# Row-wise infinity norm: another place in memory for the first tile, and a third store at the end

## The chip, the cores and the metric

The kernel runs on one core of a Trainium2 chip. The metric is the device time of one execution in microseconds (us). Before the change the median of three runs is 626.13 us (626.05 to 626.16).

## The reference

The input `x` is a matrix of 8192 x 8192 float32, 268 MB. The output is one float32 for each row, the largest absolute value in that row:

```python
return np.linalg.norm(x, ord=np.inf, axis=1)
```

Each element is read once; nothing but 32 KB is written.

## The kernel before

All arithmetic is done by VectorE: one instruction (`absmax`, L255 and L256) takes the largest absolute value along the free axis of a stretch of memory in SBUF. Everything else is loading: SyncE (SP) issues all loads, in one queue.

**Three regions of rows.** Each of the 128 partitions owns 64 rows of `x`. With `B = 2` rows a tile, a full tile is 128 partitions x 16384 elements, 64 KB a partition and 8 MB in all. Before the change the rows are split in two blocks of memory:

- The bulk, the first 38 x 128 rows. Partition p owns 38 adjacent rows, so neighbouring partitions lie 38 rows (1216 KB) apart in memory. It is loaded as 19 full tiles.
- The tail block, the last 26 x 128 rows. Partition p owns 26 adjacent rows, so neighbouring partitions lie 26 rows (832 KB) apart. Its first 24 rows are cut into 34 loads after the list `TAIL`: four full tiles, then smaller and smaller pieces down to 640 elements a partition. A piece may begin and end inside a row; then partial maxima are put in front of the piece that ends the row, and one more reduction joins them. The last 2 rows of this block (`x_f`) are the first tile of the whole kernel.

**Order.** The loop at L264 to L269 issues the first tile, then the 19 bulk tiles; the loop after L300 issues the 34 tail pieces. The tiles go round a ring of three slots in SBUF (`ring`, 3 x 16384 elements and some padding). A load into a slot waits until VectorE has reduced what was there, so at most three full tiles are in the ring. Loads are waited for with eight semaphores in rotation; a load or a store also waits for the former user of its semaphore.

**Results.** They are held in small tiles in SBUF: `r_bulk` (38 values a partition), `r_soon` (22 values, the tail's rows but its last two), and `r_late` (4 values: the tail's last two rows and the first tile's two). When the reductions of the load fourth from the end are done (L326), ScalarE issues the stores of `r_bulk` (L328) and `r_soon` (L330). SP issues the store of `r_late` (L332) after the last reduction. A tile `gap` pads the results, so that the ring begins at a multiple of 128 elements.

**Hand-made edges.** Four steps edit the finished program. `drop_implied_waits` removes waits that others imply. `start_first_load_early` puts the first load ahead of the opening barrier. `open_without_vector` takes VectorE out of that barrier. `finish_on_pool` lets GpSimd close the program: after the closing barrier it waits for the ScalarE stores' semaphores, clears the range of semaphores but for the one of the last store, waits for the last store, and resets that one by itself. It writes one clearing instruction for the semaphores below that one and one for those above; before the change none lies below. `SPARE` semaphores are allocated ahead of the others and not used; they move the numbers of the rest.

Of the kernel before, what the change touches and what calls it, by code (L numbers as in the profile page):

```python
# [12 lines left out]
F32 = mybir.dt.float32  # L13
# [4 lines left out]
HEAD, STEP = 32, 8  # L18
# [190 lines left out]
@with_exitstack  # L209
def kernel(  # L210
    ctx: ExitStack,
    tc: tile.TileContext,
    x: bass.AP,
    out: bass.AP,
    B: int = 2,
    SLOTS: int = 3,
    PAD: int = 128,
    SPARE: int = 12,
):
    nc = tc.nc  # L220
    P = nc.NUM_PARTITIONS
    rows, cols = x.shape
    W = B * cols
    R = SLOTS * W + PAD * 4


    n_tail = sum(w for _, w in TAIL) // cols
    met = 0
    for lo, w in sorted(TAIL):
        assert lo == met  # L230
        met += w
    assert met == n_tail * cols
    n_bulk_rows = rows // P - n_tail - B
    assert n_bulk_rows % B == 0
    N = n_bulk_rows // B + 1
    split = n_bulk_rows * P
    x_b = x[:split].rearrange("(p n b) c -> n p (b c)", p=P, b=B)
    out_b = out[:split].rearrange("(p n) -> p n", p=P)
    x_t = x[split:].rearrange("(p t) c -> p (t c)", p=P)
    out_t = out[split:].rearrange("(p t) -> p t", p=P)  # L240
    x_f = x_t[:, n_tail * cols :]

    for k in range(SPARE):
        nc.alloc_semaphore(f"spare{k}")
    pool = ctx.enter_context(tc.tile_pool(name="sbuf", bufs=1))
    r_bulk = pool.tile([P, n_bulk_rows], F32)
    n_soon = n_tail - 2
    r_soon = pool.tile([P, n_soon], F32)
    r_late = pool.tile([P, 2 + B], F32)
    used = [HEAD, n_bulk_rows, n_soon, 2 + B]  # L250
    gap = -sum(-(-n // STEP) * STEP for n in used) % PAD
    pool.tile([P, gap], F32, name="gap")
    ring = pool.tile([P, R], F32)

    def absmax(o, i):  # L255
        return nc.vector.reduce_max(  # L256
            out=o, in_=i, axis=X, apply_absolute_value=True
        )

    def after(ins, first, kind):  # L260
        info = mybir.DependencyInfo(kind, mybir.DependencyReason.SCHED_ONLY)
        tc.add_manual_dep(ins.ins, first.ins.name, info, reason="order")

    for n in range(N):  # L264
        at = n % SLOTS * W
        t = ring[:, at : at + W]
        nc.sync.dma_start(out=t, in_=x_f if n == 0 else x_b[n - 1])
        r = r_late[:, 2:] if n == 0 else r_bulk[:, (n - 1) * B : n * B]
        absmax(r, t.rearrange("p (b c) -> p b c", b=B))  # L269


    pieces = []
    for j, (at, w) in enumerate(TAIL):
        end = at + w
        while at < end:
            r = at // cols
            to = min(end, (r + 1) * cols)
            pieces.append((j, r, to - at))
            at = to
    of_row = [[k for k, s in enumerate(pieces) if s[1] == r] for r in range(n_tail)]  # L280


    def row_out(r):
        if r < n_soon:
            return r_soon[:, r : r + 1]
        return r_late[:, r - n_soon : r - n_soon + 1]

    here = N % SLOTS * W
    start, slot = [], []
    for j, (_, w) in enumerate(TAIL):  # L290
        first = next(s for s in pieces if s[0] == j)
        ks = of_row[first[1]]
        n_part = len(ks) - 1 if pieces[ks[-1]][0] == j else 0
        at = -(-(here + n_part) // PAD) * PAD
        if at + w > R:
            at = -(-n_part // PAD) * PAD
        start.append(at)
        slot.append(at - n_part)
        here = at + w

    for j, (src, w) in enumerate(TAIL):
        at = start[j]
        nc.sync.dma_start(out=ring[:, at : at + w], in_=x_t[:, src : src + w])
        if w == W and src % cols == 0:
            r = src // cols
            absmax(
                r_soon[:, r : r + B],
                ring[:, at : at + w].rearrange("p (b c) -> p b c", b=B),
            )
            continue  # L310
        here = [k for k, s in enumerate(pieces) if s[0] == j]
        offs = [at + sum(pieces[i][2] for i in here[:m]) for m in range(len(here))]
        todo = list(zip(here, offs))
        if slot[j] != at:

            todo = todo[1:] + todo[:1]
        for k, lo in todo:
            _, r, n = pieces[k]
            ks = of_row[r]
            if k == ks[-1]:  # L320
                frm = slot[j] if len(ks) > 1 else lo
                done = absmax(row_out(r), ring[:, frm : lo + n])
            else:
                to = slot[pieces[ks[-1]][0]] + ks.index(k)
                done = absmax(ring[:, to : to + 1], ring[:, lo : lo + n])
        if j == len(TAIL) - 4:  # L326

            ins = nc.scalar.dma_start(out=out_b, in_=r_bulk[:])  # L328
            after(ins, done, mybir.DependencyClass.Sync)
            ins = nc.scalar.dma_start(out=out_t[:, :n_soon], in_=r_soon[:])  # L330
            after(ins, done, mybir.DependencyClass.Sync)
    nc.sync.dma_start(out=out_t[:, n_soon:], in_=r_late[:])  # L332
    nc.at_finalize(drop_implied_waits)
    nc.at_finalize(start_first_load_early)
    nc.at_finalize(finish_on_pool)
    nc.at_finalize(open_without_vector)
# [30 lines left out]
```

## Time and profile before

| What | us |
|---|---|
| median of three runs | 626.13 |
| the profiled execution's own time | 626.09 |
| its span, first to last instruction | 623.5 |
| VectorE busy | 552.3 |
| VectorE waiting for loads, all groups | 70.3 |

The span is what the profile's times are counted in: 0 is the first instruction shown. A line of a group names the operation, what it writes and reads, the shape, how often, its busy time with the mean in ns, and the idle time of the engine just ahead of it with what ended that. The chain that ended last is followed back from the last instruction, at each step to what released it. For a DMA the profile gives the issue on the issuing engine's queue (SPq, ACTq) and the time from issue to landing. A window's row gives its length, the busy time of the engines, the granted TensorE clock, the mean share of the 16 DMA engines, and GB/s.

### The profile page before, as it was taken

The page shows a single profiled execution, that of the slowest core. Times are in us where ns is not written, and L with a number is a line of the kernel's source. Part 1 is how long each engine was busy: PE and PEld are TensorE (multiplying, and loading weights), DVE is VectorE, ACT ScalarE, POOL GpSimd, SP SyncE. Part 2 cuts the span into 40 slices and gives each one's busy share as a digit, 9 for nine tenths or more (in the row PEclk, how much of TensorE's full clock was granted, in tenths as well). Part 3 has the DMA queues.
Part 4 walks back from the last instruction along what each step waited for, and adds up shares of the span by engine and source line. Part 5 has one row for each costly group of instructions (what it writes and reads, how often), then busy time and mean ns, then how long its engine had stood idle before and what let it go on. Part 6 is the DMA issues. An engine that isn't in the chain of part 4 may idle for free.

```text
span 623.5 us, 152 instructions
## 1 busy us (share of the span) xinstructions
DVE 552.3 (89%) x64; POOL 0.2 (0%) x4
## 2 busy tenths in 40 slices
DVE  0588988889988899888898888988889999999999
POOL 0000000000000000000000000000000000000000
DMA  9999999999999999999999999999999999999998
GB/s 404 471 404 446 429 408 467 404 471 404 471 404 467 408 441 433 408 467 404 471 404 471 404 467 408 441 433 408 467 428 435 415 437 419 447 422 431 428 425 357
DMA packets 8065, 268.48 MB, mean 431 GB/s; under 512 B 1152, under 2 KB 1152, under 8 KB 2560
## 3 DMA queue, kind: packets, MB, share of 16 engines
q1 hardware_dynamic: 7776, 268.44, 99.7%
q10 hardware_dynamic: 288, 0.03, 0.0%
q14 instruction: 1, 0.01, 0.0%
HBM read 268.44 MB, written 0.03 MB: 431 GB/s over the span
## 4 chain that ended last, share of the span: by engine, by line
DMA 65%; DVE 35%; another core or an unknown queue 0%; issue 0%; DVEq 0%
DMA ring<-in_x_dram 65%; DVE r_bulk L256 19%; DVE r_soon L256 14%; DVE ring L256 1%; DVEq L362 0%; DVE r_late L256 0%
## 5 line engine op out<-in xcount | busy, mean ns | idle before, releaser
L256 DVE TENSOR_REDUCE r_bulk<-ring 128x2 f32<-128x16384 f32 x19 | 327.2, 17220 | 40.0 <-DMA ring<-in_x_dram 40.0
L256 DVE TENSOR_REDUCE r_soon<-ring 128x1 f32<-128x8192 f32 (+9 forms) x18 | 148.0, 8249 | 8.4 <-DMA ring<-in_x_dram 8.4
L256 DVE TENSOR_REDUCE ring<-ring 128x1 f32<-128x4992 f32 (+23 forms) x24 | 59.7, 2539 | 0.1
L256 DVE TENSOR_REDUCE r_late<-ring 128x2 f32<-128x16384 f32 (+2 forms) x3 | 18.9, 6329 | 21.9 <-DMA ring<-in_x_dram 21.9
L351 POOL MEMSET const-bfloat16-1.0<- 128x1 bf16 x1 | 0.1, 101 | 0.0
L351 POOL MEMSET const-uint8-127<- 128x1 uint8 x1 | 0.1, 101 | 0.0
L351 POOL MEMSET const-float32-0.0<- 128x1 f32 x1 | 0.1, 98 | 0.2 <-issue 0.2
L351 POOL MEMSET const-float32-1.0<- 128x1 f32 x1 | 0.1, 98 | 0.0
## 6 DMA issues: line engine op xcount, KB each, us to landing
ring<-in_x_dram SPq DMA_DIRECT2D x3, 4096.0 KB, 30.7
ring<-in_x_dram SPq DMA_DIRECT2D x2, 3744.0 KB, 38.6
ring<-in_x_dram SPq DMA_DIRECT2D x1, 6592.0 KB, 37.0
ring<-in_x_dram SPq DMA_DIRECT2D x1, 5696.0 KB, 31.1
ring<-in_x_dram SPq DMA_DIRECT2D x1, 4480.0 KB, 37.5
ring<-in_x_dram SPq DMA_DIRECT2D x1, 3328.0 KB, 42.5
ring<-in_x_dram SPq DMA_DIRECT2D x1, 2912.0 KB, 40.8
ring<-in_x_dram SPq DMA_DIRECT2D x1, 2592.0 KB, 38.3
```

The lines of the kernel that those rows point to most:

```text
L256: return nc.vector.reduce_max(out=o, in_=i, axis=X, apply_absolute_value=True)
L351: nc = _bacc.Bacc("TRN2", target_bir_lowering=False, num_devices=1)
```

## The change

The first tile is no longer taken from the end of the tail block. It is the first 256 rows of `x`: partition p takes rows 2p and 2p + 1, so the tile is one stretch of 8 MB. The bulk begins behind it and keeps 38 rows a partition. The tail block keeps only its 24 rows a partition, so that neighbouring partitions lie 24 rows (768 KB) apart. The first tile's results have a tile `r_first` and a store of their own; ScalarE issues it ahead of its two others. The final store has 2 values a partition and not 4. One spare semaphore fewer is allocated. As one more store takes a semaphore of the rotation, the final store gets the second of the eight and not the first; one semaphore then lies below it, and GpSimd's close has two clearing instructions.

```diff
-    SPARE: int = 12,
+    SPARE: int = 11,
...
-    n_bulk_rows = rows // P - n_tail - B
+    n_bulk_rows = rows // P - n_tail
     assert n_bulk_rows % B == 0
-    N = n_bulk_rows // B + 1
+    N = n_bulk_rows // B
     split = n_bulk_rows * P
-    x_b = x[:split].rearrange("(p n b) c -> n p (b c)", p=P, b=B)
-    out_b = out[:split].rearrange("(p n) -> p n", p=P)
+    x_f = x[: P * B].rearrange("(p b) c -> p (b c)", p=P)
+    out_f = out[: P * B].rearrange("(p b) -> p b", p=P)
+    x_b = x[P * B : split].rearrange("(p n b) c -> n p (b c)", p=P, b=B)
+    out_b = out[P * B : split].rearrange("(p n) -> p n", p=P)
     x_t = x[split:].rearrange("(p t) c -> p (t c)", p=P)
     out_t = out[split:].rearrange("(p t) -> p t", p=P)
-    x_f = x_t[:, n_tail * cols :]
...
-    r_bulk = pool.tile([P, n_bulk_rows], F32)
+    r_first = pool.tile([P, B], F32)
+    r_bulk = pool.tile([P, n_bulk_rows - B], F32)
...
-    r_late = pool.tile([P, 2 + B], F32)
-    used = [HEAD, n_bulk_rows, n_soon, 2 + B]
+    r_late = pool.tile([P, 2], F32)
+    used = [HEAD, B, n_bulk_rows - B, n_soon, 2]
...
-        r = r_late[:, 2:] if n == 0 else r_bulk[:, (n - 1) * B : n * B]
+        r = r_first[:] if n == 0 else r_bulk[:, (n - 1) * B : n * B]
...
         if j == len(TAIL) - 4:
 
+            ins = nc.scalar.dma_start(out=out_f, in_=r_first[:])
+            after(ins, done, mybir.DependencyClass.Sync)
             ins = nc.scalar.dma_start(out=out_b, in_=r_bulk[:])
             after(ins, done, mybir.DependencyClass.Sync)
```

## Prediction

> **What bounds the kernel now.** I read the page first: engines, DMA queues, the chain that ended last, the costliest group.
>
> ```profile
> DVE 552.3 (89%) x64; POOL 0.2 (0%) x4
> q1 hardware_dynamic: 7776, 268.44, 99.7%
> DMA 65%; DVE 35%; another core or an unknown queue 0%; issue 0%; DVEq 0%
> L256 DVE TENSOR_REDUCE r_bulk<-ring 128x2 f32<-128x16384 f32 x19 | 327.2, 17220 | 40.0 <-DMA ring<-in_x_dram 40.0
> ```
>
> The load queue keeps the 16 DMA engines busy for 99.7% of the span, VectorE is busy for 89%. In the bulk one 8 MB tile is reduced in 17.22 us, and VectorE then waits about 2.1 us (40.0 / 19) for the next load. The 35% of the chain on VectorE are no second limit: a load needs a free slot of the ring, so the chain is drawn through a reduction and then through two loads, while the queue stays full. The timeline gives the pace.
>
> ```profile
> 21.85 17.22 DVE L256 TENSOR_REDUCE r_late<-ring 128x2 f32<-128x16384 f32 x1 [21.85 <-DMA ring<-in_x_dram]
> 41.14 17.22 DVE L256 TENSOR_REDUCE r_bulk<-ring 128x2 f32<-128x16384 f32 x1 [2.07 <-DMA ring<-in_x_dram]
> ...
> 389.03 17.22 DVE L256 TENSOR_REDUCE r_bulk<-ring 128x2 f32<-128x16384 f32 x1 [2.15 <-DMA ring<-in_x_dram]
> ```
>
> Each of these reductions starts when its tile has landed, so the starts are landings. The first tile is there at 21.85, the twentieth (the last of the bulk) at 389.03: (389.03 - 21.85) / 19 = 19.33 us a tile, and 8.389 MB / 19.33 us = 434 GB/s. The end of the chain, in order of time, shows when the last load that the chain waits for is there and what is left after it:
>
> ```profile
> 609.80 11.17 DMA ring<-in_x_dram
> 620.98 0.04 issue
> 621.01 0.14 DVE r_late L256
> 621.15 0.61 issue
> 621.76 0.93 DVEq L362
> ```
>
> The tail is 24 rows a partition, as much as 12 tiles, and takes from 389.0 to 621.0: 232.0 / 12 = 19.33 us for 8 MB. So the bulk, whose partitions lie 38 rows (1216 KB) apart in memory, and the tail, whose partitions lie 26 rows (832 KB) apart, run at the same pace. A view of windows says what one row costs a DMA engine (columns: window, its length, VectorE, GpSimd, clock, DMA share, GB/s; a transfer counts whole in the window in which it starts, so a share may exceed 1):
>
> ```profile
> 0.98:1.90 0.92, 0.00 (x0) 0.00 (x0) 1.00 3.40 1140
> 60.00:80.00 20.00, 17.34 (x2) 0.00 (x0) 1.00 0.99 429
> 389.00:620.98 231.98, 223.44 (x43) 0.00 (x0) 1.00 1.00 429
> ```
>
> In the second row 429 GB/s x 20 us are 8.58 MB, or 131 pieces of 64 KB (two rows of x, what one partition takes of a tile); 0.99 x 16 engines x 20 us / 131 is 2.42 us a piece. In the first row 1140 x 0.92 is 1.05 MB, so 16 pieces, one on each engine, and 3.40 x 0.92 = 3.13 us for each. **Only the very first piece of each engine is slow**, by 0.71 us; everything later goes at the pace of an engine that never pauses.
>
> **The change, part by part.** The sum is made against the profiled execution: 626.09 us, span 623.5, so 2.6 us lie outside the span. The median of the runs is 626.13 (626.05 to 626.16); I take the 0.04 between them as nothing. About 0.2%, 1.25 us here, is what a measurement of this kernel can tell from no change.
>
> *Loads and reductions.* The same 54 loads of the same sizes in the same order, the same slots of the ring (the gap shrinks from 24 to 16 elements a partition as the results grow from 104 to 112, so the ring starts at 128 as before), the same 64 reductions with the same waits. Bytes: 268.44 MB as before, 32 tiles' worth at 19.33. Counted: 0 us. What changes is where a load reads.
>
> *First tile.* Its partitions now lie 64 KB apart, one stretch of 8 MB, and not 832 KB. No tile of the trace has this distance, so I bound it. Its landing at 21.85 follows the first issue, which the chain puts at 0.77, by 21.08 us; a tile of the full queue takes 19.33. The most that another place can give is thus 21.08 - 19.33 = 1.75 us (that also takes away the fixed way of issue and landing, which an address can hardly touch); more likely only the slow first piece, 0.71 us, depends on it. From the other side: were every piece of this tile as slow as the first, the 8 pieces of an engine would lose 7 x 0.71 = 5.0 us more. Both go straight to the end, since the queue is the limit and VectorE follows it. I take 0: 832 and 1216 KB gave the same pace, so the row nearest to it is the 2.42 us piece, and for the start the same 3.13 us.
>
> *Tail.* Its partitions lie 24 rows (768 KB) apart, not 832 KB. Not in the trace either. It can't gain: the engines were without pause at the pace that two other distances gave. The loss is bounded by the slowest piece shown: 232.0 x (3.13 / 2.42 - 1) = 68 us. I take 0, since 768 lies next to 832.
>
> [...]
>
> *The end.* ScalarE now issues three stores where it issued two, and the stores move one semaphore on. Timeline, then issue to landing:
>
> ```profile
> 620.20 0.38 ACTq L328 DMA_DIRECT2D out_dram<-r_bulk  x1
> 620.62 0.48 ACTq L330 DMA_DIRECT2D out_dram<-r_soon  x1
> 621.01 1.68 DVE L256 TENSOR_REDUCE r_late<-ring 128x1 f32<-128x773 f32 x2
> 622.72 0.35 SPq L332 DMA_DIRECT2D out_dram<-r_late  x1
> out_dram<-r_bulk ACTq DMA_DIRECT2D x1, 19.0 KB, 1.7
> out_dram<-r_soon ACTq DMA_DIRECT2D x1, 11.0 KB, 2.1
> out_dram<-r_late SPq DMA_DIRECT2D x1, 2.0 KB, 1.4
> ```
>
> Before: r_soon lands at 620.62 + 2.1 = 622.7, the final store at 622.72 + 1.4 = 624.1, which is past the span and ends the program. After: r_first at 620.20, and each later store one step of 0.42 on (620.62 - 620.20): r_bulk 620.62, r_soon 621.04, landing at 623.1; with the longer issue of 0.48 and its whole 0.48 again in landing, 623.7. That is 0.4 to 1.0 us ahead of the final store, whose issue at 622.72 hangs on VectorE alone. Behind the third store nothing is queued on ScalarE but the closing barrier, which SP joins last, after its own issue (622.72 + 0.35). The three stores wait for the earlier users of their semaphores, the loads of 1472, 1280 and 1152 elements; the reduction that releases the stores comes after all of those, so these waits are met. Its 128 pieces of 8 bytes now stand where r_bulk's 152 bytes stood beside the last load: fewer bytes, counted 0. If all cover were gone, one step would be on the path: +0.42 to +0.48. If r_first's 8-byte pieces saved the last load its company, VectorE would not notice, as it still works on the 773-element piece: no gain.
>
> *GpSimd's close.* The final store's semaphore now stands inside the range to be cleared, so there are two clearing instructions, not one. The nearest GpSimd row is
>
> ```profile
> L351 POOL MEMSET const-bfloat16-1.0<- 128x1 bf16 x1 | 0.1, 101 | 0.0
> ```
>
> 0.1 us, run while the final store is under way (1.4 us): 0, or 0.1 without that cover. Clearing comes after the waits for the other stores, at 623.1 to 623.7 by the above, so it still fits. The final store moves 8 bytes a partition, not 16, in as many pieces: between 0 and -0.1; I take 0, since 11 KB took 2.1 and 19 KB took 1.7, so bytes do not set it.
>
> **Sum:** 0 + 0 + 0 + 0 = 626.1 us, with terms of -0.7 to +0.5 that are plausible and far ends of -1.75 and +68.
>
> **Rivals.**
>
> *The first tile starts faster.* For it: 3.13 against 2.42 us is the one slow stretch of the whole queue, and the change touches its address. With 0.71 gone: 625.4, still inside 0.2%. With more than the piece gone, -1.25 to -1.75: 624.3 to 624.9. Against it: all engines start cold together whatever they read.
>
> *The third store ends the program.* r_soon's landing would have to take 1.0 us more than its 2.1. Then the close waits for it: 626.1 + 0.42 = 626.5 or so, inside 0.2%.
>
> *The tail's distance collides* (the other side). With 768 KB between partitions the engines, which step through their rows in time with each other, would ask the same part of the memory at once. It decides as soon as a 64 KB piece takes more than 2.42 us, because the load queue has no idle time to pay with. At the first tile's surplus, 1.75 us in each of 12 tiles, 647.1; at 3.13 us a piece, 626.1 + 68 = 694. Against it: neither 832 nor 1216 KB shows any of it.
>
> *The adjacent first tile collides.* Same mechanism in one tile only: up to 626.1 + 5.0 = 631.1, half of it 628.6.
>
> *The change does nothing to the addresses.* Excluded: the source distances differ in the built program.
>
> **How the numbers follow.** Forecast, 626.1: 0.42. First piece at full pace, 625.4: 0.12. Third store on the path, 626.5: 0.10. These three are within 0.2%: 0.64. First tile gains over 1.25: 0.10, so faster 0.10. Tail collides: 0.16; first tile collides: 0.10; slower 0.26. [...] The range goes from 624.3, the far end of the gain, to 628.6, half of the first tile's loss: 0.64 + 0.10 + about 0.05 = 0.79.
>
> **What would show it.** Right: first landing near 21.85, bulk and tail at 19.33 us for 8 MB, r_soon landed before the final store, ends within a few tenths. A first landing below 21.2 shows the faster start. Wrong: a tail that takes more than 233 us from the last bulk landing, with VectorE idle ahead of its r_soon groups; a first landing past 22.5; a final store that is not the last to land.

## The result, and the profile after

The changed kernel takes 627.39 us (median of 16 runs, 626.86 to 628.05), the kernel before 626.15 beside it (16 runs, 625.97 to 626.40). The ratio is 1.0021, with a 95% interval of 1.0014 to 1.0027: **slower by about 1.2 us**. The runs also scatter over 1.2 us, where those of before scatter over 0.4. The profiled execution took 627.54 us, 1.45 more than that of before, and its span is the same 623.5 us. So the loss lies past the last instruction shown. The other runs say the same: the time less the span is 3.2 to 4.4 us in the sixteen runs, and 2.6 to 2.7 in every run of the kernel before that was timed beside the experiments below.

The loads first, in the same windows as before the change:

```profile
0.98:1.90 0.92, 0.00 (x0) 0.00 (x0) 1.00 3.30 1140
60.00:80.00 20.00, 17.27 (x2) 0.00 (x0) 1.00 0.99 429
389.00:620.98 231.98, 223.42 (x43) 0.00 (x0) 1.00 1.00 429
```

A piece of 64 KB still takes 2.42 us, the first one of each engine 3.30 x 0.92 = 3.04 us where it took 3.13, and the tail has its 429 GB/s (the columns are window, length, VectorE, GpSimd, clock, share of the DMA engines, GB/s). The timeline agrees: landings at 21.97 and 389.05, where they were at 21.85 and 389.03.

```profile
21.97 17.22 DVE L258 TENSOR_REDUCE r_first<-ring 128x2 f32<-128x16384 f32 x1 [21.97 <-DMA ring<-in_x_dram]
...
389.05 17.22 DVE L258 TENSOR_REDUCE r_bulk<-ring 128x2 f32<-128x16384 f32 x1 [2.15 <-DMA ring<-in_x_dram]
```

The end, as issues on the queues (start, length) and as times from issue to landing:

```profile
620.22 0.38 ACTq L330 DMA_DIRECT2D out_dram<-r_first  x1
620.64 0.44 ACTq L332 DMA_DIRECT2D out_dram<-r_bulk  x1
621.03 1.68 DVE L258 TENSOR_REDUCE r_late<-ring 128x1 f32<-128x773 f32 x2
621.12 0.49 ACTq L334 DMA_DIRECT2D out_dram<-r_soon  x1
622.74 0.35 SPq L336 DMA_DIRECT2D out_dram<-r_late  x1
```

```profile
out_dram<-r_bulk ACTq DMA_DIRECT2D x1, 19.0 KB, 3.8
out_dram<-r_first ACTq DMA_DIRECT2D x1, 1.0 KB, 3.3
out_dram<-r_soon ACTq DMA_DIRECT2D x1, 11.0 KB, 4.2
out_dram<-r_late SPq DMA_DIRECT2D x1, 1.0 KB, 2.9
```

The issues stand where the prediction put them, within 0.1 us. The landings do not: r_bulk went from 1.7 to 3.8, r_soon from 2.1 to 4.2, and the final store from 1.4 to 2.9. It now lands at 622.74 + 2.9 = 625.6 and not at 624.1. These 1.5 us are the whole of the 1.45. The final store comes from SP's queue, not ScalarE's, moves half the bytes that it moved before, and is issued at the same time; that it is late because of a store ahead of it is what the experiments show. In the trace's records its sixteen engines used to report between 623.97 and 624.14; now the first does at 623.99 and the last at 625.59, 1.45 later.

So the lateness is not kept to one queue: the store on SP's took 2.9 us instead of 1.4. But a mere wait for r_first does not give the amount: r_first has landed at 620.22 + 3.3 = 623.5, and the three stores behind it land 0.9, 1.8 and 2.1 us after that.

### The profile page after: what moved, and what is told of

Same layout as the page of the kernel before. It is cut to its first block, busy times and chain, and to the rows that moved or that the text cites. A ratio compares the mean times of both kernels' runs of the same rounds, so it can differ in the third digit from the quotient of the medians.

```text
span 623.5 us, 153 instructions
## 1 busy us (share of the span) xinstructions
DVE 552.3 (89%) x64; POOL 0.2 (0%) x4
## 4 chain that ended last, share of the span: by engine, by line
DMA 65%; DVE 35%; another core or an unknown queue 0%; issue 0%; DVEq 0%
DMA ring<-in_x_dram 65%; DVE r_bulk L258 19%; DVE r_soon L258 14%; DVE ring L258 1%; DVEq L366 0%; DVE r_late L258 0%
## 5 line engine op out<-in xcount | busy, mean ns | idle before, releaser
L258 DVE TENSOR_REDUCE r_first<-ring 128x2 f32<-128x16384 f32 x1 | 17.2, 17220 | 22.0 <-DMA ring<-in_x_dram 22.0
L258 DVE TENSOR_REDUCE r_late<-ring 128x1 f32<-128x773 f32 (+1 forms) x2 | 1.7, 884 | 0.0
```

What stands on the lines that cost most here:

```text
L258: return nc.vector.reduce_max(out=o, in_=i, axis=X, apply_absolute_value=True)
```

## The experiments

All were timed beside the kernel before, whose median was 626.10 to 626.18 each time. The landings shown are those of one profiled execution, the medians those of 5 to 11 runs. Theory D came from the profile after: the store of r_first, 128 pieces of 8 bytes one behind the other in 1 KB, is slow to land and holds up what follows. The rivals were the number of stores (N) and the changed addresses (A).

**no_first_store: the store taken out.** The changed kernel without it (the first 256 results are not written), with `SPARE` at 12 again:

```diff
-            ins = nc.scalar.dma_start(out=out_f, in_=r_first[:])
-            after(ins, done, mybir.DependencyClass.Sync)
```

> The changed kernel without the store of r_first (256 of the 8192 results are not written); loads, addresses and the tail of 24 rows stay as changed; the close is again one clearing instruction. Theory D (the 128 pieces of 8 bytes that lie one behind the other in 1 KB are slow to land, and the stores behind them wait with them): r_bulk, r_soon and the final store land after 1.7, 2.1 and 1.4 us as before the change, median 626.1 to 626.3. Theory N (a third store as such is too many at the end): the same, 626.1 to 626.3. Theory A (addresses: 768 KB tail, adjacent first tile, a final store of 8 bytes at a distance of 96): the landings stay late, 627.2 to 627.6.

```profile
out_dram<-r_bulk ACTq DMA_DIRECT2D x1, 19.0 KB, 1.7
out_dram<-r_soon ACTq DMA_DIRECT2D x1, 11.0 KB, 2.4
out_dram<-r_late SPq DMA_DIRECT2D x1, 1.0 KB, 1.4
```

626.19 us, ratio 0.9999 (0.9990 to 1.0008), and the old landings but for 0.3 us in r_soon. The adjacent first tile, the tail of 24 rows and the final store of 8 bytes stay in and cost nothing that can be seen. A falls.

**extra_dense and extra_104: the store added to the kernel before, dense or spread.** Both send the first tile's two values of each partition to a scratch tensor, ahead of r_bulk's store; only the distance of the pieces differs (`n` is 2 or 26 elements; `SPARE` is 11, as after the change):

```diff
+    scratch = nc.dram_tensor("scratch", (P, n), F32).ap()
...
+            ins = nc.scalar.dma_start(out=scratch[:, :B], in_=r_late[:, 2:])
+            after(ins, done, mybir.DependencyClass.Sync)
             ins = nc.scalar.dma_start(out=out_b, in_=r_bulk[:])
```

> The kernel before, with a third ScalarE store ahead of the two: the first tile's two values of each partition, 8 bytes, go once more to a scratch tensor of 1 KB, one behind the other. Theory D: as after the change, landings of 3 us and more, median 627.0 to 627.7. Theory N: the same. Theory A: 626.1 to 626.3, since no load and no piece of the final store moves.

```profile
out_dram<-r_bulk ACTq DMA_DIRECT2D x1, 19.0 KB, 5.2
scratch<-r_late ACTq DMA_DIRECT2D x1, 1.0 KB, 3.3
out_dram<-r_soon ACTq DMA_DIRECT2D x1, 11.0 KB, 5.1
out_dram<-r_late SPq DMA_DIRECT2D x1, 2.0 KB, 3.8
```

> As the kernel with the dense extra store, but the 128 pieces of 8 bytes lie 104 bytes apart in the scratch tensor. Theory D: the third store lands within about 2 us, nothing behind it waits, median 626.1 to 626.4. Theory N (the number of stores): 627.0 to 627.7, as with the dense one. Theory A: 626.1 to 626.3.

```profile
out_dram<-r_bulk ACTq DMA_DIRECT2D x1, 19.0 KB, 2.2
scratch<-r_late ACTq DMA_DIRECT2D x1, 1.0 KB, 1.7
out_dram<-r_soon ACTq DMA_DIRECT2D x1, 11.0 KB, 1.8
out_dram<-r_late SPq DMA_DIRECT2D x1, 2.0 KB, 1.4
```

Dense: 627.91 us, ratio 1.0030 (1.0018 to 1.0041), with the loads of before. Spread: 626.19, ratio 1.0000 (0.9991 to 1.0008). Same number of stores, same 1 KB, same position, same two clearing instructions at the close. N falls, and with it every cost of the third store as such. So the dense place of the pieces is the cause: with everything else alike, it alone makes the stores behind late. The dense one loses even more than the change did (1.7 against 1.2 us); the landings shown for it are those of an execution of 628.61 us, above the median.

**first_last: the order of the three stores.** r_first's store is issued behind r_bulk's and r_soon's.

> The changed kernel with the store of r_first as the last of the three on ScalarE, not the first. Theory D: r_bulk and r_soon land after 1.7 to 2.1 us again, r_first, issued at 621.1, after 3 us or more, at 624.2 to 624.5, so the close waits for it or for the final store that stands behind it on the same DMA engines: 626.5 to 627.6. Theory N: the third of the three is the late one whatever it writes, 627.0 to 627.6. Theory A: 627.2 to 627.6, unchanged.

```profile
out_dram<-r_bulk ACTq DMA_DIRECT2D x1, 19.0 KB, 1.7
out_dram<-r_soon ACTq DMA_DIRECT2D x1, 11.0 KB, 2.1
out_dram<-r_first ACTq DMA_DIRECT2D x1, 1.0 KB, 3.8
out_dram<-r_late SPq DMA_DIRECT2D x1, 1.0 KB, 2.6
```

626.80 us, ratio 1.0011 (1.0002 to 1.0019); the landings are those of the slowest of the eleven runs (627.42). What stands ahead of the dense store is as quick as before the change, what stands behind it (the final store, 2.6) is not: the delay goes down the line only.

**first_early: the same store 580 us before the end**, right behind the first tile's reduction and no longer at the end:

```diff
         absmax(r, t.rearrange("p (b c) -> p b c", b=B))
+        if n == 0:
+            nc.scalar.dma_start(out=out_f, in_=r_first[:])
```

> The changed kernel with the dense store of r_first issued by ScalarE right after the first tile's reduction, some 580 us before the end; two ScalarE stores are left at the end, and the final store of 8 bytes. Theory D: the dense store is as slow to land (3 us or more) but nothing stands behind it, so the end is as before: r_bulk 1.7, r_soon 2.1, final store 1.4 us, median 626.1 to 626.4; some of it may be lost to the loads that share the DMA engines, at most about 0.3. Rival: the close with two clearing instructions, or the changed rotation of semaphores, costs the time: 627.0 and more.

```profile
out_dram<-r_bulk ACTq DMA_DIRECT2D x1, 19.0 KB, 1.7
out_dram<-r_first ACTq DMA_DIRECT2D x1, 1.0 KB, 21.8
out_dram<-r_soon ACTq DMA_DIRECT2D x1, 11.0 KB, 2.2
out_dram<-r_late SPq DMA_DIRECT2D x1, 1.0 KB, 1.4
```

The end is as before the change, with two clearing instructions and the shifted semaphores, so those cost nothing. The median is 626.61, ratio 1.0006 (0.9997 to 1.0014; runs from 626.07 to 627.11), 0.2 above what D had allowed and not told apart from no change. In all eleven runs the time is 2.6 to 2.7 us more than the span, as before the change, so what is above it lies in the span (623.4 to 624.5), in the loads and not at the end. The store now shares the DMA engines with the loads: it takes 21.8 us to land. The load that is under way comes 19.57 us after the one before it instead of 19.34, and the next one makes it up (19.16 instead of 19.40):

```profile
41.05 17.22 DVE L258 TENSOR_REDUCE r_bulk<-ring 128x2 f32<-128x16384 f32 x1 [2.09 <-DMA ring<-in_x_dram]
60.62 17.22 DVE L258 TENSOR_REDUCE r_bulk<-ring 128x2 f32<-128x16384 f32 x1 [2.35 <-DMA ring<-in_x_dram]
79.78 17.22 DVE L258 TENSOR_REDUCE r_bulk<-ring 128x2 f32<-128x16384 f32 x1 [1.95 <-DMA ring<-in_x_dram]
```

The profiled execution took 626.21, less than the median. What the longer ones lose in their loads it does not show.

**in_bulk: the tail of 24 rows and the 8-byte final store alone.** The first tile is an ordinary bulk tile (40 rows a partition), its results a part of r_bulk, and there is no third store.

> The tail of 24 rows and the final store of 8 bytes alone: the first tile is an ordinary bulk tile (40 rows a partition, 1280 KB apart), its results are part of r_bulk, and ScalarE has two stores, the first of 160 bytes a partition. Theory D: 626.1 to 626.3, bulk and tail at 19.33 us a tile. Theory A (addresses of the loads or the final store's 8 bytes cost something): above 626.5.

626.42 us, ratio 1.0005 (0.9996 to 1.0014): not told apart from before, though it lies between what D and what A had expected, and all eleven runs (626.33 to 626.73) are above the median of before. The landings are 1.7, 2.1 and 1.4 us and the time less the span is 2.6 in every run, so the end is as before. The bulk in this run, at 1280 KB, takes (389.36 - 22.15) / 19 = 19.33 us a tile.

**extra_64 and extra_32: how far apart is far enough.** As extra_104, with other distances.

> The kernel before with the extra store of 128 pieces of 8 bytes, 64 bytes apart. [...] Theory R (all 128 pieces in a region of a few KB crowd one place of the memory, whatever their distance): 8 KB is still small, landing between that of 1 KB (3.3 us) and of 13 KB (1.7), median 626.4 to 627.7.

> The same with 32 bytes between the pieces, two in each 64 bytes, 4 KB in all. [...] Theory R: later than with 64 bytes, 2.3 us and more, median 626.6 to 627.8.

626.16 and 626.15 us, both with a ratio of 1.0000 (0.9991 to 1.0009). Even 32 bytes are free, the whole store lying in 4 KB:

```profile
out_dram<-r_bulk ACTq DMA_DIRECT2D x1, 19.0 KB, 2.1
scratch<-r_late ACTq DMA_DIRECT2D x1, 1.0 KB, 1.7
out_dram<-r_soon ACTq DMA_DIRECT2D x1, 11.0 KB, 1.8
out_dram<-r_late SPq DMA_DIRECT2D x1, 2.0 KB, 1.4
```

So a small region as such (R) is not it, by which 4 KB would be later than 8: the extra store lands after 1.7 us with either. And two pieces in one stretch of 64 bytes cost nothing here (r_bulk 2.1 and r_soon 1.8 us, against 2.2 and 1.8 with 104 bytes).

**extra_16 and dense_16B: between 8 and 32.** Pieces of 8 bytes at a distance of 16, and pieces of 16 bytes without a gap.

> The kernel before with the extra store of 128 pieces of 8 bytes, 16 bytes apart, two in each 32 bytes. Theory S (pieces that share an aligned stretch of 32 bytes must be written one after the other; a distance of 32 bytes was free): two share instead of four, so it lands between 1.7 and 3.3 us, say 2.0 to 2.8, median 626.3 to 627.3. Theory X (only pieces of several DMA engines in one stretch of 64 bytes collide, or it takes four in one): free, 1.7 us, 626.1 to 626.3.

> The same, but each piece is 16 bytes long (four values of r_bulk), so the pieces lie one behind the other in 2 KB without a gap. Theory S: as with 8 bytes at 16 bytes of distance, two to a stretch of 32 bytes, 626.3 to 627.3. A theory that it is density (no gap between pieces) and not sharing: as late as the dense 8 bytes, 627.0 to 628.

```profile
out_dram<-r_bulk ACTq DMA_DIRECT2D x1, 19.0 KB, 2.9
scratch<-r_late ACTq DMA_DIRECT2D x1, 1.0 KB, 1.7
out_dram<-r_soon ACTq DMA_DIRECT2D x1, 11.0 KB, 2.9
out_dram<-r_late SPq DMA_DIRECT2D x1, 2.0 KB, 1.5
```

626.32 (ratio 1.0006, 0.9997 to 1.0014; runs up to 627.23) and 626.17 (1.0001, 0.9993 to 1.0010). The landings shown are extra_16's, and dense_16B's are like them (1.7, 2.9, 2.7, 1.4): the two stores behind are late by about 1 us, but they still end by 624.0, ahead of the final store, and the end barely moves. That is so in most runs only: in five of extra_16's eleven, from 626.46 up, the time is 3.0 to 3.8 us more than the span and not 2.6, so there the lateness reaches the end. Lack of gaps alone is not the cause, as 16-byte pieces have none and lose no more. The lateness begins between 32 and 16 bytes of distance and reaches the end of the program in every run only at 8.

**dense_32p, dense_16p and dense_127p: whose pieces collide.** The dense extra store with fewer partitions:

> The dense extra store with 32 partitions only, 32 pieces of 8 bytes in 256 bytes, two on each of the 16 DMA engines. Theory S: still four in each 32 bytes, but a quarter as many; if the lateness is a queue of collisions at one place of the memory it falls to about a quarter of 1.6 us, landing 2.0 to 2.3 us, median 626.1 to 626.7. If a collision has a fixed price whatever the number, landing stays at 3 us and the median at 627 and more.

```profile
out_dram<-r_bulk ACTq DMA_DIRECT2D x1, 19.0 KB, 4.2
scratch<-r_late ACTq DMA_DIRECT2D x1, 0.2 KB, 3.2
out_dram<-r_soon ACTq DMA_DIRECT2D x1, 11.0 KB, 5.1
out_dram<-r_late SPq DMA_DIRECT2D x1, 2.0 KB, 3.9
```

628.24 us, ratio 1.0033 (1.0021 to 1.0045). A quarter of the pieces is as late as all of them: not the queue of collisions by which it would have landed after 2.0 to 2.3 us, but a price that does not grow with the number from 32 to 128.

> The dense extra store with 16 partitions: 16 pieces of 8 bytes in 128 bytes, one on each DMA engine, so that pieces next to each other always come from different engines. Theory E (writes of different engines into one short stretch collide, and each engine's later stores wait behind): landing 3 us or more, median 627.2 to 628.5. Theory O (an engine's own consecutive pieces in one stretch collide): landing 1.7, median 626.1 to 626.3.

> The dense extra store with 127 partitions. As 127 has no divisor up to 16 but 1, all pieces should go to one DMA engine, if the trace shows it so; then no two engines share a stretch. Theory E: no collision, the one engine is busy some 1.1 us (127 pieces of about 9 ns) longer; landing about 2.8, median 626.1 to 626.6. Theory O: the one engine has all the collisions, landing 4 us or more, median 627.5 and up.

dense_16p: 626.31 us, ratio 1.0003 (0.9994 to 1.0012). Its eleven runs reach from 626.05 to 627.45, and in the two slowest the time is about 3.5 us more than the span, so pieces that the expectation gives to different engines are not wholly harmless. The profiled one was the slowest: the extra store itself landed in 1.7 us, the final one in 2.3, and the rest of its surplus is 0.4 us of span. dense_127p: 629.08 us, ratio 1.0045 (1.0032 to 1.0057), the slowest of all:

```profile
out_dram<-r_bulk ACTq DMA_DIRECT2D x1, 19.0 KB, 4.9
scratch<-r_late ACTq DMA_DIRECT2D x1, 1.0 KB
out_dram<-r_soon ACTq DMA_DIRECT2D x1, 11.0 KB, 5.2
out_dram<-r_late SPq DMA_DIRECT2D x1, 2.0 KB, 3.9
```

The extra store has no landing in this view; in the trace's records its semaphore moves only twice, just after the issue and at 625.43, where those of the other stores move sixteen times, once for each engine. So a single engine had work to report. The counts of records on ScalarE's queue say the same: 288 with two stores of 128 pieces (256 pieces and 16 reports for each store), 144 more with a third of 128 (432 in extra_dense), 48 more with 32 pieces (336), 32 more with 16 (320), and here 128 more (416), which is 127 pieces and one report. These counts are all that the runs show of how pieces are dealt to engines; a rule by divisors is the author's reason, and no run tests it further. The one engine had begun its last piece at 621.88, so its writes were pending for 3.5 us more, and no second engine writes there. So small writes into one short stretch are late without a second engine, as theory O has it, and E is not needed. No run spreads the pieces of a single engine, so how much of the 3.5 us comes from the short stretch, and how much from 127 pieces on one engine, is not shown.

## Why the prediction was wrong

- *Loads and reductions, first tile, tail, all at 0*: right. 768 KB of distance runs at the pace of 832 and 1216 (429 GB/s in the tail), the tile at 64 KB lands no later, with both of them no_first_store takes 626.19, and in_bulk adds 1280. The two colliding rivals, 0.26 together and the only ones counted as slower, did not happen: the kernel is slower for another reason. No run shows a distance that collides, to which the forecast gave 0.16 for the tail: at 768, 832, 1216 and 1280 KB 8 MB take 19.33 us.
- *The first tile starts faster*: no. The first piece went from 3.13 to 3.04 us, against 2.42 for a later one at either place, and the landing from 21.85 to 21.97. That is scatter: in the profiled executions the landing lies between 21.82 and 22.15 with the old place of the tile (before, extra_dense, extra_104, extra_64, extra_32) and between 21.73 and 22.06 with the new one (after, no_first_store, first_last, first_early).
- *The order of issues at the end*: right within 0.1 us. That the waits of the three stores are met, and that the close hides its second clearing instruction: right (extra_104 and first_early have both).
- **The step that failed is "The end"**: "the longer issue of 0.48 and its whole 0.48 again in landing, 623.7". r_soon landed at 621.12 + 4.2 = 625.3, and the final store, counted at an unchanged 1.4, took 2.9. The mistake was to take the landing time of the new store, and of everything behind it, from stores of 152, 88 and 16 bytes a piece that do not lie dense at that size. The words "fewer bytes, counted 0" and "bytes do not set it" were used as a reason for no cost, when the distance of the pieces was new as well and no row showed it. The size is not what costs: 8-byte pieces at 104 bytes land in 1.7 us and delay nothing. The distance is: at 8 bytes the same store makes all that stands behind it late.
- *The rival "the third store ends the program"* had the right place and side, at 626.5; its price was one step of 0.42, and the measured one is 1.2 (1.45 in the profiled execution). Its condition, 1.0 us more than 2.1 for r_soon, was met twice over. But the end is not one store waiting its turn: all stores behind the dense one are late, the final one on SP's queue too, and that one lands last.
- The median lies inside the range, but by luck: the upper end, 628.6, was there for a collision of the first tile's loads, which did not happen. The kernel is slower beyond its interval, where no change was forecast.

That the dense place is the cause is shown; how it works is not. What stays open: why 32 pieces are as late as 128; why r_bulk and r_soon are later still in extra_dense (5.2 and 5.1 us) than in the changed kernel (3.8 and 4.2); why they are late in extra_16 (2.9 both), where the extra store itself lands after 1.7 us like a spread one; and what makes such writes slow. Their size alone does not explain it: 8-byte pieces 32 bytes apart land in 1.7 us.

## What to carry to other kernels

A small store is not priced by its bytes or by its place in the queue alone: look at how its pieces lie in memory. Here, at the end of the program, 8-byte pieces, 32 or more of them one behind the other, made the stores behind them 1.2 to 3.5 us late, on another queue too, and 32 bytes from the start of one piece to the start of the next took that away. When a program's end is a chain of short stores, let small results ride along in a wider piece: before the change the first tile's went out in the 16-byte pieces of the final store, in in_bulk in the 160-byte pieces of r_bulk, and neither has a late landing (1.4 and 1.7 us). Spreading the pieces is possible only where their places are free, as in the scratch tensor here; the output's are not. And look past the end of the span, where the landings are.

## What had not been expected

- A store of 256 bytes in 32 pieces cost 2.1 us of program time (628.24 against 626.18) and landed after 3.2 us, while one of 19 KB that lies dense in pieces of 152 bytes landed in 1.7 before the change.
- Between loads, the same dense store lands after 21.8 us and costs 0.5 at the median (626.61 against 626.15, not told apart from no change), all of it in the span, against 1.2 us at the end.
- Four distances between partitions (768, 832, 1216 and 1280 KB) give the same pace of loading, 19.33 us for 8 MB, and a single tile at 64 KB is no exception that can be seen.
